# Second attention of a two-layer encoder: three small moves in the order of its steps

## The chip, the cores and the metric

The kernel runs on one core of a Trainium2 chip. The metric is device time in microseconds (us). The core has a matrix engine (PE, with its weight loads as PEld), a vector engine (DVE), a scalar engine (ACT), a general engine (POOL) and queues that issue transfers (DMAs), here nearly all on SP. Each engine runs its own instructions in order, and semaphores hold an instruction until what it needs is done. Matrix products land in PSUM, eight banks of 128 x 512 f32; everything else on chip lies in SBUF.

## The reference

Two layers act on x of 1024 tokens by 1024. Layer 0 is dilated window attention. Layer 1, where the change lies, is latent attention with 16 heads (64 plus 32 rotary columns for the scores, 64 for the values):

```python
    cq, ckv, k_rope, gate = jnp.split(
        u @ w_in, [Q_LORA_RANK, Q_LORA_RANK + KV_LORA_RANK, Q_LORA_RANK + KV_LORA_RANK + QK_ROPE_DIM], axis=-1)
    q = (rmsnorm(cq, q_norm) @ w_uq).reshape(B, S, N_HEADS_B, QK_NOPE_DIM + QK_ROPE_DIM)
...
    kv = (rmsnorm(ckv, kv_norm) @ w_ukv).reshape(B, S, N_HEADS_B, QK_NOPE_DIM + V_HEAD_DIM)
...
    q_rope = rope(q_rope, cos[:, None], sin[:, None])
    k_rope = rope(k_rope, cos, sin)
...
        s = (jnp.einsum('bqhd,bkhd->bhqk', qn, k_nope)
             + jnp.einsum('bqhd,bkd->bhqk', qr, k_rope)).astype(jnp.float32) * scale
        p = jax.nn.softmax(s, axis=-1).astype(v.dtype)
        return jnp.einsum('bhqk,bkhd->bqhd', p, v)
...
    y = o * jax.nn.silu(gate)
    return y @ w_out
```

After each layer x becomes LayerNorm(sqrt(2) * x + gate_c * mixer(u)).

## The kernel before

Every f32 operand of a product is split into a high part (fp32r) and a low part, and a product is three matmuls: high by high, low by high, high by low (`mm3`, lines 93 to 95). A split is a cast on ACT (high) and a subtraction on DVE or POOL (low).

`layer_b_attention` sweeps 64 work items, w = 0 to 63, in one loop with two more turns (w = 64 = `nw`, and 65). One turn is a cycle: w // 4 is the head, w // 8 = p the pair of heads, r = w % 8 the place in the pair. A cycle holds 256 queries of a head as two halves a. In each cycle PE does in this order: scores of half 0 (`full`, `small`, into `s`), the transposes of the previous item's probabilities (`turned`, into `t`), scores of half 1, transposes again, any up-projection (into `m`), and last `values(w - 2)`, the product with V (into `o`). DVE does: `osum` of the previous cycle, the row maximum `mb` of half 0 (line 1452), two low splits `ptl` (line 1491), `mb` of half 1, two more `ptl`. ACT does the high splits `pth`, the exponentials `pr`, and the copy of `o` to `osum` (line 1525). POOL multiplies the result into `gT` (line 1529) and, for every second cycle, by the reciprocal of the softmax denominator (`normalise`, line 1535), which travels through DRAM (`den_d`, `rden`, lines 1515 and 1516).

The order on PE, SP, ACT and DVE is the order in which the code is written; only POOL's is chosen by a scheduler. Four PSUM banks (`mbank`: `t`, `m` and `o`) turn in a ring: each allocation waits until the one four before it has been read. So `values(w - 2)`, and an up-projection in front of it, wait until DVE has done the first `ptl` of the same cycle or the second.

`b_weights(p)` splits the up-projection weights of pair p: a cast to `wuh` on ACT (line 1210), a subtraction to `wul` on POOL (line 1211), and then `b_wload(p + 1)` queues the next raw weights on SP (line 1197, `wuraw`), which overwrite the tile that the split has read. Pair p + 2 is split at r = 7 of pair p. For p + 2 even its first reader is `b_turn` (rotary part) at r = 0 of the next pair, one cycle later; its rotary product is multiplied on DVE (line 1334, `ab`) by tables `tab` that `b_tabs(0)` queues on SP at r = 7 (line 1315). For p + 2 odd the first reader comes at r = 3.

In the last pair (p = 7) the output weights are loaded and split: `b_wo_split(r - 1)` for r = 1 to 4 with its low part on POOL (`wl`, line 106, 128 x 1024). `b_yt(b, 0)` splits a tile of y^T: a cast on ACT (line 1649) and a subtraction on DVE whose two inputs both lie in SBUF (line 1650, `ytb`). Tiles 0, 1, 2 are split at r = 5, 6, 7, tile 3 and 4 in cycle 64. `b_out_blocks(i, blocks)` adds products of y^T and output weights into output rows i (`po`), 6 matmuls a block. In cycle 64 the four blocks of i = 0 stand so: block 0, transposes, block 1, transposes' splits, `values(62)`, blocks 2 and 3; then cycle 65 has `values(63)`.

Of the kernel before, what the change touches and what calls it, by code (L numbers as in the profile page):

```python
# [28 lines left out]
NPAIR_B = 8  # L29
# [41 lines left out]
class Trunk:  # L71
# [1349 lines left out]
    def layer_b_attention(self):  # L1421
# [4 lines left out]
        def full(w, a):  # L1426

            hd, t = w // 4, 2 * (w % 4)
            (qa, qb, q3), k = self.q[hd], self.kb[hd % 3]
            ts = slice((t + a) * P, (t + a) * P + P)  # L1430
            for n, (q, kk) in enumerate(((qa, k[0]), (qb, k[1]))):
                for j in range(2):
                    ks = slice(j * 512, j * 512 + 512)
                    nc.tensor.matmul(sc[w][a][:, ks], q[:, ts], kk[:, ks], start=n == a == 0, stop=n == a == 1)  # L1434
            if a and w % 4 == 3:
                self.q.pop(hd)

        def small(w):

            hd, t = w // 4, w % 4  # L1440
            q3 = self.q[hd][2]
            for g in range(4):
                rows = slice(32 * g, 32 * g + 32)
                ks = slice((g % 2) * 512, (g % 2) * 512 + 512)
                nc.tensor.matmul(  # L1445
                    sc[w][g // 2][:, ks], q3[rows, t * P : t * P + P], self.kr[rows, :],
                    start=g >= 2, stop=g < 2, tile_position=(32 * g, 0),
                )

        def maximum(w, a):  # L1450
            m = mx[w, a] = self.M.tile([P, 4], F32, tag="mb", bufs=4, name=self.nm("mb"))
            nc.vector.tensor_reduce(m[:, 0:1], sc[w][a], axis=AX.X, op=ALU.max, negate=True)  # L1452

        def expo(w, a):
            hd, t = w // 4, 2 * (w % 4) + a
            if t == 0:
                dens[hd] = self.M.tile([P, 8], F32, tag="den", bufs=3, name=self.nm("den"))
            pr = prs[w, a] = self.ht(F32, "pr")
            nc.scalar.activation(  # L1459
                pr, sc[w][a], AF.Exp, bias=mx.pop((w, a))[:, 0:1], accum_out=dens[hd][:, t : t + 1]  # L1460
            )
            if a:
                sc.pop(w)

        def reciprocal(w):
            d = dens[w // 4][:, 2 * (w % 4) - 2 : 2 * (w % 4) + 2]
            nc.vector.reciprocal(d, d)

        def turned(w, a):
            pr = prs.pop((w, a))  # L1470
            tb[w, a] = []
            for j in range(2):
                t = self.mbank("t")
                for c in range(4):
                    kt = 4 * j + c
                    nc.tensor.transpose(t[:, c * P : c * P + P], pr[:, kt * P : kt * P + P], self.ident)  # L1476
                tb[w, a].append(t)
# [4 lines left out]
        def high(w, a):  # L1482
            if a == 0:
                pts[w] = [(self.gt(F32R, "pth"), self.gt(F32R, "ptl")) for _ in range(2)]
            for j in range(2):
                nc.scalar.copy(part(w, a, j, 0), tb[w, a][j].rearrange("p (k q) -> p k q", k=4))  # L1486

        def low(w, a):
            for j, t in enumerate(tb.pop((w, a))):
                src = t.rearrange("p (k q) -> p k q", k=4)  # L1490
                nc.vector.tensor_tensor(part(w, a, j, 1), src, f32(part(w, a, j, 0)), op=ALU.subtract)  # L1491

        def values(w):
            hd = w // 4
            po = ob[w] = self.mbank("o")
            x = [(kt, x) for kt in range(8) for x in range(2)]
            for n, (kt, i) in enumerate(x):
                v = self.vq[hd // 4][kt // 2][:, (kt % 2) * 512 + (hd % 4) * P : (kt % 2) * 512 + (hd % 4) * P + P]
                c = (kt % 4) * 256
                nc.tensor.matmul(po[:, 0:256], v, pts[w][kt // 4][i][:, c : c + 256], start=n == 0, stop=n == 15)  # L1500
            pts.pop(w)
            if w % 16 == 15:
                self.vq.pop(hd // 4)
            if w % 2:
                nc.tensor.transpose(po[0:4, 256:384], dens[hd][:, 2 * (w % 4) - 2 : 2 * (w % 4) + 2], self.ident)
# [25 lines left out]
        def normalise(v):  # L1531
            hd = v // 2
            mine = slice(64 * (hd % 2), 64 * (hd % 2) + 64)
            g = self.gT[hd // 2][mine, v % 2 * 512 : v % 2 * 512 + 512]
            nc.gpsimd.tensor_tensor(g, g, rden.pop(v)[mine, :], op=ALU.mult)  # L1535
# [5 lines left out]
        for w in range(nw + 2):  # L1541
            p, r = divmod(w, 8)
            now, old = w < nw, 1 <= w <= nw
            more = p + 1 < NPAIR_B
            if now:
                sc[w] = [self.PB.tile([P, 1024], F32, tag="s", bufs=2, name=self.nm("s")) for _ in range(2)]
                full(w, 0)
                small(w)
            if w == nw:
                self.b_out_blocks(0, range(1))  # L1550
            if old:
                turned(w - 1, 0)
            if now:
                maximum(w, 0)
            if old:
                high(w - 1, 0)
                low(w - 1, 0)
                if w % 2 == 0:
                    reciprocal(w - 1)
            if now:  # L1560
                expo(w, 0)
                full(w, 1)
                maximum(w, 1)
            if old:
                turned(w - 1, 1)
                high(w - 1, 1)
                low(w - 1, 1)
            if r == 7 and p % 2 == 0 and p + 2 < NPAIR_B:
                self.tabs = {}
                self.b_tabs(0)  # L1570
            if r == 0 and p % 2 and more:
                self.b_tabs(1)

            splits = []
            if p % 2 == 0 and now and r < 2:
                splits += [self.b_v(p // 2, j) for j in (2 * r, 2 * r + 1)]
            if more and r == 3:
                self.b_heads(p + 1)
            if more and 3 <= r <= 6:
                splits.append(self.b_qk(p + 1, "kqkq"[r - 3], (r - 3) // 2))  # L1580
            if more and p % 2 and r < 2:
                turn, store = self.b_turn(p + 1, r)
                splits.append(turn)
                rot.append((w + 1, store))
            late = splits.pop() if w >= 8 and r == 1 and p % 2 == 0 and splits else None
            if w >= 2:
                for f in splits:
                    f()
            if now:
                expo(w, 1)  # L1590
            if w < 2:
                for f in splits:
                    f()
            if more and r == 5:
                self.b_rotary(p + 1)
            if w == nw:
                self.b_out_blocks(0, range(1, 2))
            if w >= 2:
                values(w - 2)
                output(w - 2)  # L1600
            if late:
                late()

            while rot and rot[0][0] <= w:
                rot.pop(0)[1]()
            if w == 1:
                self.b_weights(1)
            if r == 7 and p + 2 < NPAIR_B:
                self.b_weights(p + 2)
            if r == 5 and p % 2 and more:  # L1610
                self.b_vweights((p + 1) // 2)
            if p == 7:
                if r < 4:
                    self.b_wo_load(r)
                if 1 <= r <= 4:
                    self.b_wo_split(r - 1, nc.gpsimd)
                if r >= 5:
                    self.b_yt(r - 5, 0)
                if r == 7:
                    for b in range(4, 8):  # L1620
                        self.b_wo_load(b)
            if w == nw:
                self.b_yt(3, 0)
                self.b_rows()
                self.b_out_blocks(0, range(2, 4))
                for b in (4, 5):
                    self.b_wo_split(b, nc.vector)
                    if b == 4:
                        self.b_yt(b, 0)
            if w == nw + 1:  # L1630
                self.b_out_blocks(1, range(4))
            if w >= 5 and w % 2:
                normalise((w - 5) // 2)
# [225 lines left out]
```

## Time and profile before

| what | us |
|---|---|
| median of 3 runs (1326.19 to 1332.42) | 1326.89 |
| the profiled execution's own time | 1328.96 |
| its span | 1327.2 |
| PE busy with matmuls in the span | 1305.0 (98%) |
| DVE / ACT / POOL busy | 858.4 / 745.8 / 392.4 |

The second attention runs from about 760 us to 1235 us of the span, the output products from there to the end. TensorE's granted clock is full (1.00) in all of it. The busy share says little here: with PE at 98% only what PE waits for can be gained, and what makes it wait longer is lost.

### The profile page before, as it was taken

The numbers are of one execution on the slowest core, as the hardware profiler recorded it, in microseconds if no ns is written. First come the engines' busy times: TensorE is split into PE (matmuls) and PEld (weight loads), VectorE is DVE, ScalarE is ACT, GpSimd is POOL, SyncE is SP. The second block draws the span as 40 slices with busy tenths as digits, with TensorE's granted clock in tenths as the row PEclk, the third lists the DMA queues.
The fourth block names the chain that finished last, engine by engine and source line by source line (L and its number), as shares of the span: only waits on it lengthen the run. The fifth ranks groups of instructions, "written<-read, shape, count | busy, mean of one in ns | idle before, by whom it ended". The sixth has DMA issues, their size and how long they took to land.

```text
span 1327.2 us, 20680 instructions
## 1 busy us (share of the span) xinstructions
PE 1305.0 (98%) x7435; PEld 1100.5 (83%) x7435; DVE 858.4 (65%) x1502; ACT 745.8 (56%) x1519; POOL 392.4 (30%) x399
## 2 busy tenths in 40 slices
PE   9999999999999999999999999999999999999997
PEld 6888888888888888888998878788888888878886
DVE  7654445445445435646754358888888888878896
ACT  5665456554443432435742277777777777778521
POOL 0332133223222267702742101521332142124200
PEclk9999999999999999999999999999999999999999
DMA  9413121113243246545134124462552544340531
GB/s 366 159 31 70 29 64 40 48 40 113 77 148 130 91 124 167 191 150 185 61 114 133 41 69 108 122 154 57 138 131 66 134 120 116 70 126 26 215 127 64
DMA packets 71967, 146.45 MB, mean 110 GB/s; under 512 B 11148, under 2 KB 25789, under 8 KB 71864
## 3 DMA queue, kind: packets, MB, share of 16 engines
q1 hardware_dynamic: 69196, 139.75, 35.7%
q0 software_dynamic: 2048, 5.06, 1.1%
q8 instruction: 59, 0.97, 0.3%
q14 instruction: 44, 0.36, 0.1%
q10 hardware_dynamic: 620, 0.31, 0.1%
HBM read 107.96 MB, written 12.87 MB: 91 GB/s over the span
## 4 chain that ended last, share of the span: by engine, by line
PE 87%; DVE 4%; DMA 4%; ACT 2%; issue 1%; POOL 1%; SPq 0%; ACTq 0%; DVEq 0%; POOLq 0%
PE pj L93 9%; PE pj L95 9%; PE pj L94 9%; PE o L1500 9%; PE s L1434 7%; PE t L1476 7%; PE po L95 5%; PE po L93 5%; PE po L94 5%; PE ip L274 2%; PE t L577 2%; PE pg L93 2%; PE s L1445 2%; PE pg L95 2%; PE pg L94 2%; DVE mb L1452 2%
## 5 line engine op out<-in xcount | busy, mean ns | idle before, releaser
L93 PE MATMUL pj<-uh,wh 128*128 128x512 f32 x528 | 217.2, 411 | 0.7 <-ACT wh L105 0.7
L95 PE MATMUL pj<-uh,wl 128*128 128x512 f32 x528 | 207.1, 392 | 0.0
L94 PE MATMUL pj<-ul,wh 128*128 128x512 f32 x528 | 206.8, 392 | 0.0
L1486 ACT CAST pth<-t 128x512 fp32r<-128x512 f32 x256 | 137.9, 597 | 63.0 <-PE t L1476 62.6
L1452 DVE TENSOR_REDUCE mb<-s 128x1 f32<-128x1024 f32 x128 | 155.2, 1213 | 16.3 <-PE s L1445 15.3
L1491 DVE TENSOR_TENSOR ptl<-t,pth 128x512 fp32r<-128x512 f32 x256 | 164.1, 682 | 1.5 <-ACT pth L1486 0.5
L1459 ACT ACTIVATE pr<-s,mb 128x1024 f32<-128x1024 f32 x128 | 144.9, 1132 | 8.7 <-DVE mb L1452 7.3
L1434 PE MATMUL s<-kb,q 128*128 128x512 f32 x512 | 147.9, 410 | 0.0
L1476 PE MATMUL t<-ident,pr 128*128 128x128 f32 x1024 | 136.2, 276 | 0.7 <-DVE osum L1528 0.7
L106 POOL TENSOR_TENSOR wl<-wraw,wh 128x1024 fp32r<-128x1024 f32 x42 | 106.3, 2537 | 99.3 <-ACT wh L105 73.4
L1476 PEld LDWEIGHTS t<-ident,pr 128*128 128x128 f32 x1024 | 114.5, 141 | 24.8 <-issue 9.1
L1500 PE MATMUL o<-pth,vq 128*128 128x256 f32 x512 | 127.7, 287 | 3.4 <-DVE ptl L1491 3.0
L1500 PE MATMUL o<-ptl,vq 128*128 128x256 f32 x512 | 125.2, 283 | 0.0
L566 ACT ACTIVATE sb<-sb,stat 128x256 f32<-128x256 f32 (+1 forms) x144 | 67.0, 466 | 95.8 <-DVE stat L560 95.7
L95 PEld LDWEIGHTS pj<-uh,wl 128*128 128x128 f32 x528 | 99.1, 188 | 22.2
L93 PEld LDWEIGHTS pj<-uh,wh 128*128 128x128 f32 x528 | 99.7, 189 | 15.1 <-ACT wh L105 1.1
L94 PEld LDWEIGHTS pj<-ul,wh 128*128 128x128 f32 x528 | 99.8, 189 | 13.9
L1500 PEld LDWEIGHTS o<-pth,vq 128*128 128x128 f32 x512 | 97.2, 190 | 7.0 <-DVE ptl L1491 5.5
L1500 PEld LDWEIGHTS o<-ptl,vq 128*128 128x128 f32 x512 | 97.5, 190 | 1.6
L1434 PEld LDWEIGHTS s<-kb,q 128*128 128x128 f32 x512 | 87.0, 189 | 12.6 <-issue 0.2
L1529 POOL TENSOR_TENSOR gT<-osum,gT 64x256 f32<-64x256 f32 x64 | 46.6, 728 | 161.1 <-DVE osum L1528 159.6
L1535 POOL TENSOR_TENSOR gT<-gT,rden 64x512 f32<-64x512 f32 x32 | 41.7, 1302 | 145.8 <-DMA rden<-den_d 135.4
(288 smaller groups left out, 2766.7 us busy)
## 6 DMA issues: line engine op xcount, KB each, us to landing
wraw<-wa SPq DMA_DIRECT2D x36, 512.0 KB
ada<-ada_row SPq DMA_DIRECT2D x64, 256.0 KB
kb<-hl SPq DMA_DIRECT2D x84, 128.0 KB
q<-hl SPq DMA_DIRECT2D x84, 128.0 KB
wraw<-wo_a SPq DMA_DIRECT2D x18, 512.0 KB
ada<-ada_ss SPq DMA_DIRECT2D x16, 512.0 KB
f<-f_d SPq DMA_DIRECT2D x18, 256.0 KB
xr<-x SPq DMA_DIRECT2D x8, 512.0 KB
```

Of the source, the lines that this page charges most:

```text
L93: mm(out, wh, xh, start=start, stop=False)
L94: mm(out, wh, xl, start=False, stop=False)
L95: mm(out, wl, xh, start=False, stop=stop)
L106: (lo_engine or self.nc.gpsimd).tensor_tensor(l[:, :width], raw[:, :width], f32(h[:, :width]), op=ALU.subtract)
L566: nc.scalar.activation(sb[:, a * w : a * w + w], sb[:, a * w : a * w + w], AF.Exp, bias=stat[:, 0, hh, t : t + 1], scale=-1.0, accum_out=s ...
L1434: nc.tensor.matmul(sc[w][a][:, ks], q[:, ts], kk[:, ks], start=n == a == 0, stop=n == a == 1)
L1452: nc.vector.tensor_reduce(m[:, 0:1], sc[w][a], axis=AX.X, op=ALU.max, negate=True)
L1459: nc.scalar.activation(pr, sc[w][a], AF.Exp, bias=mx.pop((w, a))[:, 0:1], accum_out=dens[hd][:, t : t + 1])
L1476: nc.tensor.transpose(t[:, c * P : c * P + P], pr[:, kt * P : kt * P + P], self.ident)
L1486: nc.scalar.copy(part(w, a, j, 0), tb[w, a][j].rearrange("p (k q) -> p k q", k=4))
L1491: nc.vector.tensor_tensor(part(w, a, j, 1), src, f32(part(w, a, j, 0)), op=ALU.subtract)
L1500: nc.tensor.matmul(po[:, 0:256], v, pts[w][kt // 4][i][:, c : c + 256], start=n == 0, stop=n == 15)
```

## The change

Three things move, and nothing is computed more or less. (1) The weights of pair p + 2 are split at r = 6, one cycle sooner. (2) `b_yt` of tiles 0 to 3 comes at r = 4 to 7 of the last pair, tile 4 in cycle 64 ahead of the splits of the output weights. (3) In cycle 64 blocks 1 and 2 stand in front of `values(62)`, block 3 behind it.

```diff
             if w == nw:
-                self.b_out_blocks(0, range(1, 2))
+                self.b_out_blocks(0, range(1, 3))
...
-            if r == 7 and p + 2 < NPAIR_B:
+            if r == 6 and p + 2 < NPAIR_B:
                 self.b_weights(p + 2)
...
-                if r >= 5:
-                    self.b_yt(r - 5, 0)
+                if r >= 4:
+                    self.b_yt(r - 4, 0)
...
             if w == nw:
-                self.b_yt(3, 0)
+                self.b_yt(4, 0)
                 self.b_rows()
-                self.b_out_blocks(0, range(2, 4))
+                self.b_out_blocks(0, range(3, 4))
                 for b in (4, 5):
                     self.b_wo_split(b, nc.vector)
-                    if b == 4:
-                        self.b_yt(b, 0)
```

The built programs show where the instructions land. POOL, cycles 5 to 7 (pair 0; `wul` is the split of pair 2, the two gT<-gT,rden are `normalise`), before:

```order
L1535 TENSOR_TENSOR gT_6064<-gT_6064,rden_7214 64x512
L1529 TENSOR_TENSOR gT_6064<-osum_7309,gT_6064 64x256
L1529 TENSOR_TENSOR gT_6064<-osum_7390,gT_6064 64x256
L1211 TENSOR_TENSOR wul_7399<-wuraw_6846,wuh_7398 128x640
L1535 TENSOR_TENSOR gT_6064<-gT_6064,rden_7392 64x512
```

and now:

```order
L1535 TENSOR_TENSOR gT_6064<-gT_6064,rden_7214 64x512
L1529 TENSOR_TENSOR gT_6064<-osum_7309,gT_6064 64x256
L1211 TENSOR_TENSOR wul_7314<-wuraw_6846,wuh_7313 128x640
L1529 TENSOR_TENSOR gT_6064<-osum_7396,gT_6064 64x256
L1535 TENSOR_TENSOR gT_6064<-gT_6064,rden_7398 64x512
```

The split has moved ahead of one multiplication, not ahead of the `normalise` before it. In pairs 2 and 4 it moves ahead of a `normalise` too. SP at the same place (`wuraw` is the raw weights of pair 3, `tab` the tables of cycles 8 and 9), before:

```order
L1394 DMA q_6980<-hl_7281 64x512
L1315 DMA tab_7365<-qtab 64x512 x4
L1515 DMA den_d<-rden_7392 4x128
L1516 DMA rden_7392<-den_d 64x512
L1197 DMA wuraw_7402<-wu_o 128x384
L1315 DMA tab_7459<-qtab 64x512 x4
```

and now:

```order
L1394 DMA q_6980<-hl_7281 64x512
L1197 DMA wuraw_7317<-wu_o 128x384
L1315 DMA tab_7371<-qtab 64x512 x4
L1515 DMA den_d<-rden_7398 4x128
L1516 DMA rden_7398<-den_d 64x512
L1315 DMA tab_7459<-qtab 64x512 x4
```

The load of raw weights, which waits for the split on POOL, now stands in front of the first tables. DVE from the end of cycle 60 (`osum` is its last instruction there, `mb` and `ptl` belong to cycle 61), before:

```order
L1528 TENSOR_TENSOR osum_12355<-o_12338,osum_12355 64x256
L1452 TENSOR_REDUCE mb_12383<-s_12363 128x1
L1491 TENSOR_TENSOR ptl_12386<-t_12373,pth_12385 128x4x128
L1491 TENSOR_TENSOR ptl_12388<-t_12378,pth_12387 128x4x128
L1452 TENSOR_REDUCE mb_12399<-s_12364 128x1
```

and now:

```order
L1528 TENSOR_TENSOR osum_12355<-o_12338,osum_12355 64x256
L1648 TENSOR_TENSOR ytb_12363<-gT_6064,ytb_12363 128x512
L1452 TENSOR_REDUCE mb_12386<-s_12366 128x1
L1491 TENSOR_TENSOR ptl_12389<-t_12376,pth_12388 128x4x128
L1491 TENSOR_TENSOR ptl_12391<-t_12381,pth_12390 128x4x128
L1452 TENSOR_REDUCE mb_12402<-s_12367 128x1
```

A y^T split stands in front of the first maximum of cycle 61, where there was none; cycles 62 and 63 begin with such a split in both programs. On ACT the matching cast stands behind the cast of the fourth output weights.

## Rows read from the trace of the kernel before

**Rows 1.** What PE waited for, 826 to 1240 us: total, times, longest.

```profile
PE o L1500 <- DVE ptl L1491: 2.8, 6, 1.3
PE m L95 <- POOL wul L1211: 1.3, 1, 1.3
PE t L1476 <- DVE osum L1528: 0.7, 1, 0.7
PE po L95 <- DVE ytb L1650: 0.4, 1, 0.4
```

**Rows 2.** Timeline, cycle 8's rotary product: start, us, engine, line, [idle before <- releaser].

```profile
834.33 0.40 PE L94 MATMUL m<-latl,wuh 128*128 128x512 f32 x1
...
836.03 0.19 PEld L95 LDWEIGHTS m<-lath,wul 128*128 128x128 f32 x1 [1.73 <-POOL wul L1211]
836.03 0.50 PE L95 MATMUL m<-lath,wul 128*128 128x512 f32 x1 [1.30 <-POOL wul L1211]
...
836.60 0.39 PE L94 MATMUL m<-latl,wuh 128*128 128x512 f32 x1
...
836.83 0.39 PE L95 MATMUL m<-lath,wul 128*128 128x512 f32 x1
```

**Rows 3.** Line 1211's own view: weight loads that waited for it (us, times).

```profile
  PEld m L95: 2.6, 3
```

**Rows 4.** Timeline of POOL, 831 to 836 us.

```profile
831.58 1.28 POOL L1535 TENSOR_TENSOR gT<-gT,rden 64x512 f32<-64x512 f32 x1 [13.15 <-DMA rden<-den_d]
832.93 1.43 POOL L1529 TENSOR_TENSOR gT<-osum,gT 64x256 f32<-64x256 f32 x2
834.44 1.54 POOL L1211 TENSOR_TENSOR wul<-wuraw,wuh 128x640 fp32r<-128x640 f32 x1
```

**Rows 5.** Timelines of SP, DVE, PE, cycles 7 to 9; then windows (last: DMA share, GB/s).

```profile
832.92 2.52 SPq L1315 DMA_DIRECT2D tab<-qtab  x4
...
837.26 1.29 DVE L1334 TENSOR_TENSOR ab<-m,tab 128x512 f32<-128x512 f32 x2 [0.55 <-PE m L95]
...
841.79 1.29 DVE L1491 TENSOR_TENSOR ptl<-t,pth 128x512 fp32r<-128x512 f32 x2
...
843.08 0.47 PE L93 MATMUL m<-lath,wuh 128*128 128x512 f32 x1
...
837.00:837.50 0.50, 0.50 (x5) 0.46 (x5) 0.24 (x1) 0.00 (x0) 0.00 (x0) 1.00 0.00 0
```

**Rows 6.** Timeline at the turn from cycle 60 to cycle 61.

```profile
1206.19 1.06 ACT L105 ACTIVATE wh<-woraw 128x1024 fp32r<-128x1024 f32 x1
...
1206.89 1.22 DVE L1452 TENSOR_REDUCE mb<-s 128x1 f32<-128x1024 f32 x1 [0.25 <-PE s L1445]
1207.41 2.39 POOL L106 TENSOR_TENSOR wl<-woraw,wh 128x1024 fp32r<-128x1024 f32 x1
...
1209.44 0.36 PE L1500 MATMUL o<-pth,vq 128*128 128x256 f32 x1
```

**Rows 7.** Timelines of POOL and DVE behind the heads: the two splits meet.

```profile
1239.72 2.49 POOL L106 TENSOR_TENSOR wl<-woraw,wh 128x1024 fp32r<-128x1024 f32 x1 [0.33 <-ACT wh L105]
...
1240.14 2.62 DVE L1650 TENSOR_TENSOR ytb<-gT,ytb 128x512 fp32r<-128x512 f32 x1 [0.21 <-ACT ytb L1649]
```

**Rows 8.** Timeline of cycle 62, which begins with a y^T split already.

```profile
1211.79 0.37 ACT L1525 COPY osum<-o 64x256 f32<-64x256 f32 x1
...
1213.13 1.17 DVE L1650 TENSOR_TENSOR ytb<-gT,ytb 128x512 fp32r<-128x512 f32 x1 [0.18 <-ACT ytb L1649]
...
1216.08 0.39 PE L1500 MATMUL o<-pth,vq 128*128 128x256 f32 x1 [0.19 <-DVE ptl L1491]
...
1219.08 0.36 ACT L1525 COPY osum<-o 64x256 f32<-64x256 f32 x1
```

**Rows 9.** Timeline of PE, block 3 in cycle 64.

```profile
1233.39 0.40 PE L94 MATMUL po<-wl,ytb 128*128 128x512 f32 x1
...
1234.23 0.50 PE L95 MATMUL po<-wh,ytb 128*128 128x512 f32 x1 [0.44 <-DVE ytb L1650]
```

## The prediction, made blind

> **What bounds the kernel.** I read what PE waited for first, over the stretch that the change touches. The view is short: the waits add up to 5.2 us in 414 us [rows 1]. So PE sets the end, and the change can give back no more than the waits it removes. Two of the four rows are its targets: the wait of an up-projection for the weight split `wul` (1.3 us) and that of an output block for a y^T split (0.4 us). A third row, `values` waiting for `ptl`, is the one that the change can make longer, since what is put on DVE in front of `mb` delays `ptl`. Next I read the timelines around each of the three places, to see which engine is late and what is queued there.
>
> **Part 1, weights one cycle sooner.** The price in the trace: the matmul of line 95 starts 1.70 us after the one of line 94, where the undisturbed pitch is 0.23 (836.60 to 836.83), so 1.47 us are lost in cycle 8 [rows 2]. The weight load there stood idle 1.73, and 0.26 of that cost nothing. All three such loads (pairs 2, 4 and 6) idled 2.6 us [rows 3]; the other two share 0.87, of which 2 x 0.26 cost nothing, so 0.35 us.
>
> What is won in those two: there the split moves ahead of a `normalise` and is ready a whole cycle sooner, so I take the 0.35 whole. In cycle 8 it is different. POOL did not start `wul` late because ACT was late, but because it stood 13.15 us in front of a `normalise` whose `rden` came late from DRAM [rows 4]. The new order puts `wul` ahead of one multiplication only, and that `normalise` is still in front. Its DMA is issued ahead of everything that moves, so it lands as before. The split gains one multiplication, half of 1.43: it ends at 835.2 instead of 835.98, and PE gains 0.74 of its 1.47.
>
> What is added: the raw-weight load moves past four `tab` loads on SP and waits for that same split. Behind it are queued the tables for cycle 8. They began at 832.92 and took 0.63 each to issue; now the load starts at 835.2, the tables at about 835.85. The fourth began its issue at 834.8 and no DMA moved anything from 837.0 on, so it landed within 2.2 us [rows 5]. Now the second lands at 838.7, the fourth at 839.9, and DVE's pair of multiplications, which began at 837.26 when the product was there, ends at 840.55 instead of 838.55. Behind it stand `osum` (256 columns; about 0.4, an estimate from the 0.65 of a `ptl` of 512), `mb` (1.22) and the first `ptl` (0.65) [rows 5, 6]: done at about 842.8. The next product on PE needs that bank; it began at 843.08, now it could at 842.34, so it waits about 0.5. Net gain in cycle 8: 0.2. Bounds: 1.47 gained if nothing of this counts, 2.0 lost if the late tables and what follows them on SP hold POOL and then ACT as in the worst such place of the trace, where a 0.7 and a 1.3 us wait on PE stand next to each other [rows 1].
>
> The cast on ACT also moves. In cycle 60 a longer cast (1.06 us) stands in the same place, in front of the next `pth`, and PE's `values` behind it began without a wait [rows 6]. So it costs nothing; if that gap were full it would cost at most that 1.06 in each of six cycles. In pairs 3, 5 and 7 the split has no reader for cycles: nothing won, nothing lost.
>
> **Part 2, one more y^T split within the heads.** Four splits now stand within the heads, not three, and the added one comes at the end of cycle 60. That is the cycle in which POOL makes its last `wl` split, 1207.41 to 1209.80 [rows 6]. The ACT cast for y^T stands behind the ACT cast for `wh`, which also releases POOL; so POOL is always first. What happens then is seen once in the trace: POOL began such a split at 1239.72, DVE a y^T split at 1240.14, and that took 2.62 us, ending 0.55 after POOL's (1242.76 and 1242.21) [rows 7]. In cycle 62 the same instruction took 1.17 [rows 8]. I read it as DVE held until POOL is through. The Trainium skill says so too (page "SBUF — State Buffer", section "Who interferes with whom"): a DVE instruction with two SBUF inputs and a GpSimd instruction that reads SBUF exclude each other for the whole of the first, and whoever issues first goes first. By that rule the sum below stands; were the 2.62 a chance delay of ACT's, it would be the first rival.
>
> So the added split ends at 1209.80 + 0.55 = 1210.35. Behind it on DVE wait `mb`, which began at 1206.89, and `ptl`. In cycle 62 `values` began 1.78 us after its split's end (1214.30 to 1216.08), and ACT's copy to `osum` at the end of that cycle 4.78 after it (1219.08) [rows 8]. So cycle 61's `values` begin at 1212.13 instead of 1209.44: PE stands 2.7 us. And ACT's copy, on which cycle 62's chain hangs, comes at 1215.13 instead of 1211.79, 3.3 us later. Cycles 62 and 63 have the split in both kernels and are already bound by this chain (PE waits there), so they pass the 3.3 on and give nothing back. Bounds: 0 if all of it hides, 3.5 if `mb` itself sets the rest (1210.35 less 1206.89).
>
> **Part 3, cycle 64.** Block 3 waited for its y^T tile: 0.84 between two matmuls where 0.23 is the pitch, 0.6 lost [rows 9]. Tile 3 is now split a cycle sooner, and block 3 comes behind `values(62)`: I take the 0.6 whole. Blocks 1 and 2 need tiles split in cycles 61 and 62. The same matmuls run in another order, at no cost. DVE has one y^T split less between 1233 and 1237, so the output weights behind it are no later.
>
> **The sum**, against the profiled execution (1328.96, of it 1327.2 span): +3.3 - 0.6 - 0.35 - 0.2 = +2.1 us, 1331.1. That execution stands 2.07 above the median of the runs; on the median of 1326.89 it is 1329.0. About 0.5%, 6.6 us, is what a measurement of this kernel can tell from no change, so this is "the same".
>
> **The rivals.**
> First, DVE is not held: the added split starts when ACT's cast is done (`wh` ends at 1207.25, a cast half as wide adds about 0.5: 1207.8), and takes the 1.17 of its neighbours. It ends at 1209.0, ACT's copy comes at 1213.8, 2.0 late: +2.0 - 1.15 = +0.85, 1327.7. For it: other splits within the heads are not long. Against it: none of them meets a `wl` on POOL.
> Second, faster: the added split hides, and all three weight waits go: -1.47 - 0.35 - 0.6 = -2.4, 1324.5. For it: in cycle 61 PE did not wait for DVE. Against it: cycles 62 and 63 did as soon as they had such a split.
> Third, SP becomes the one that is late: the held load makes tables, denominators and rotary rows late after cycle 8 and costs 2.0 there instead of the gain of 0.2: +4.3, 1331.2. For it: SP's DMAs stand back to back there. Against it: DVE and PE have slack in a cycle with a product.
> Fourth, over the bound: in pairs 1, 3 and 5 the two weight loads now also stand in front of a denominator. If each late denominator holds POOL, and so ACT, at 2.0 as in the worst place, that is three times 2.0 on top of the third rival: +10.3, 1337.2. It decides if POOL takes a `normalise` ahead of a multiplication that ACT's tile needs; POOL's new order does not do that there.
>
> **The numbers.** Forecast 0.5, first rival 0.2, second 0.1, third 0.15, fourth 0.05. The range takes in the forecast, the first and third rival and half of the second, with a run's scatter of about 1 us: 1325.2 to 1332.0. Faster by over 0.5% needs more than all shown waits: 0.01. Slower by over 0.5% is the fourth rival: 0.05. The rest, 0.94, is the same.
>
> **What would show it.** Right: a y^T split of about 2.5 us near 1207.8 that ends just behind POOL's `wl`, and behind it a wait of PE's `values` for `ptl` of 2 to 3 us in cycle 61; a wait for `wul` in cycle 8 that shrinks but stays, near 0.6; none in pairs 4 and 6; no wait of an output block for `ytb`; DVE's multiplication by `tab` in cycle 8 beginning 1 to 2 us after its product. Wrong: a short split there, or a `values` of cycle 61 without a wait (part 2); no wait for `wul` at all, or a new one of ACT for POOL in cycles 8 to 10 (part 1).

## The result, and the profile after

| what | before | after |
|---|---|---|
| median of 20 runs each, us | 1329.35 (1326.19 to 1332.97) | 1332.17 (1329.43 to 1336.52) |
| ratio after to before, 95% interval | 1 | 1.0022 (1.0014 to 1.0031) |
| the profiled execution's own time, us | 1328.96 | 1330.68 |
| its span, us | 1327.2 | 1328.9 |

The changed kernel is slower by 2.9 us (1.9 to 4.1), 0.2% and so within the 0.5% called "the same". The forecast of a difference was +2.1. The forecast of a time, 1329.0 with a range up to 1332.0, was too low: the median of the kernel before, which it was set on, rose from 1326.89 in three runs to 1329.35 in twenty.

The waits of PE over 826 to 1240 us, as in [rows 1]:

```profile
PE o L1500 <- DVE ptl L1491: 5.7, 7, 2.4
PE m L93 <- DVE ptl L1491: 1.0, 1, 1.0
PE m L95 <- POOL wul L1211: 0.6, 1, 0.6
```

The wait for `ytb` is gone, and so is the one of a transpose for `osum`. The wait for `wul` has halved. In their place stand 2.9 us more of `values` waiting for `ptl`, and an up-projection that waits 1.0.

**Cycle 8** (answers [rows 2] and [rows 4]), timelines of PE and POOL:

```profile
834.44 0.40 PE L94 MATMUL m<-latl,wuh 128*128 128x512 f32 x1
835.41 0.50 PE L95 MATMUL m<-lath,wul 128*128 128x512 f32 x1 [0.57 <-POOL wul L1211]
```

```profile
831.65 1.27 POOL L1535 TENSOR_TENSOR gT<-gT,rden 64x512 f32<-64x512 f32 x1 [13.11 <-DMA rden<-den_d]
833.00 0.73 POOL L1529 TENSOR_TENSOR gT<-osum,gT 64x256 f32<-64x256 f32 x1
833.82 1.55 POOL L1211 TENSOR_TENSOR wul<-wuraw,wuh 128x640 fp32r<-128x640 f32 x1
```

POOL still stands 13.11 us in front of `normalise`. The split now follows one multiplication instead of two, ends at 835.37, and PE's step from line 94 to line 95 is 0.97 us instead of 1.70. **Cycle 9** pays for it (answers [rows 5]); timelines of SP, DVE, PE:

```profile
835.39 0.37 SPq L1197 DMA_DIRECT2D wuraw<-wu_o  x1
835.86 2.43 SPq L1315 DMA_DIRECT2D tab<-qtab  x4
```

```profile
839.14 0.69 DVE L1334 TENSOR_TENSOR ab<-m,tab 128x512 f32<-128x512 f32 x1 [2.37 <-DMA tab<-qtab]
840.50 0.69 DVE L1334 TENSOR_TENSOR ab<-m,tab 128x512 f32<-128x512 f32 x1 [0.67 <-DMA tab<-qtab]
```

```profile
843.68 0.50 PE L93 MATMUL m<-lath,wuh 128*128 128x512 f32 x1 [0.98 <-DVE ptl L1491]
```

SP holds the raw load until the split has ended (835.39), the tables begin 2.9 us later than before (835.86 against 832.92), and DVE waits for them twice. Windows of a quarter of a us (the last two columns are the share of the DMA engines and GB/s) show when the tables' last bytes moved:

```profile
839.75:840.00 0.25, 0.25 (x6) 0.20 (x3) 0.08 (x1) 0.00 (x0) 0.00 (x0) 1.00 0.07 17
840.00:840.25 0.25, 0.25 (x4) 0.25 (x4) 0.00 (x0) 0.00 (x0) 0.00 (x0) 1.00 0.00 0
```

No transfer moved anything from 840.00 on, and yet DVE went on only at 840.50.

**Cycles 60 and 61** (answers [rows 6]), timelines of POOL, DVE, PE:

```profile
1206.67 2.37 POOL L106 TENSOR_TENSOR wl<-woraw,wh 128x1024 fp32r<-128x1024 f32 x1
```

```profile
1206.96 2.63 DVE L1648 TENSOR_TENSOR ytb<-gT,ytb 128x512 fp32r<-128x512 f32 x1 [1.06 <-ACT ytb L1647]
1209.52 1.21 DVE L1452 TENSOR_REDUCE mb<-s 128x1 f32<-128x1024 f32 x1
```

```profile
1211.38 0.39 PE L1500 MATMUL o<-pth,vq 128*128 128x256 f32 x1 [2.36 <-DVE ptl L1491]
1218.61 0.39 PE L1500 MATMUL o<-pth,vq 128*128 128x256 f32 x1 [0.76 <-DVE ptl L1491]
```

The added y^T split lasts 2.63 us, ends at 1209.59, 0.55 after POOL's `wl` (1209.04), and `values` of cycle 61 stands 2.36. In cycle 64 the matmuls of block 3 follow each other at 0.23 (answers [rows 9]):

```profile
1235.60 0.40 PE L93 MATMUL po<-wh,ytb 128*128 128x512 f32 x1
1235.83 0.40 PE L94 MATMUL po<-wl,ytb 128*128 128x512 f32 x1
1236.07 0.39 PE L95 MATMUL po<-wh,ytb 128*128 128x512 f32 x1
```

**Where the difference sits, cycle by cycle.** From the timeline of PE I took the start of the small scores (line 1445) in each cycle. The table has the length from one such start to the next, in us, of each kernel's profiled execution; all cycles left out agree within 0.3. "Start" is where cycle 0 begins, "rest" what follows the start of cycle 63. The runs are explained below; the first two have the same instruction order.

| kernel | start | 8 | 9 | 24 | 26 | 40 | 56 | 57 | 61 | 62 | rest |
|---|---|---|---|---|---|---|---|---|---|---|---|
| before | 778.7 | 9.06 | 7.60 | 7.86 | 6.10 | 7.68 | 8.65 | 6.21 | 6.20 | 6.56 | 108.1 |
| norm_later | 778.4 | 9.05 | 7.60 | 8.50 | 6.48 | 8.51 | 8.45 | 6.20 | 6.20 | 6.55 | 108.0 |
| after | 778.8 | 8.33 | 8.86 | 7.50 | 6.10 | 7.50 | 7.92 | 6.21 | 8.83 | 7.13 | 107.3 |
| after_again | 777.7 | 7.97 | 8.75 | 7.50 | 7.26 | 7.50 | 7.85 | 6.21 | 10.36 | 6.52 | 107.3 |
| weights_only | 777.7 | 7.97 | 8.88 | 7.51 | 6.10 | 7.50 | 7.79 | 6.21 | 6.20 | 6.56 | 108.1 |
| load_late | 778.5 | 7.74 | 7.60 | 7.51 | 6.10 | 7.50 | 9.85 | 6.22 | 6.21 | 6.56 | 108.1 |
| yt_only | 779.9 | 9.28 | 7.60 | 7.73 | 6.38 | 8.32 | 9.75 | 6.21 | 10.22 | 6.56 | 107.3 |
| yt_first | 781.0 | 9.85 | 7.60 | 7.53 | 6.10 | 7.99 | 7.75 | 6.20 | 6.50 | 7.13 | 107.2 |
| yt_early | 778.1 | 8.88 | 7.60 | 8.05 | 6.10 | 8.35 | 8.04 | 7.20 | 6.21 | 6.54 | 107.3 |
| pool_yt | 781.6 | 8.57 | 7.60 | 7.50 | 7.18 | 7.51 | 7.76 | 6.20 | 6.21 | 6.10 | 106.3 |
| pool_fixed | 779.4 | 7.51 | 7.58 | 7.51 | 6.93 | 7.50 | 6.10 | 6.20 | 6.21 | 6.50 | 108.1 |
| best | 781.0 | 7.50 | 7.59 | 7.51 | 6.14 | 7.51 | 6.10 | 6.21 | 6.20 | 6.10 | 106.2 |
| best_old_weights | 778.1 | 7.50 | 7.59 | 7.51 | 7.43 | 7.51 | 6.10 | 6.21 | 6.21 | 6.10 | 106.3 |
| after_fixed | 779.5 | 7.50 | 7.72 | 7.51 | 6.10 | 7.50 | 6.10 | 6.21 | 10.28 | 6.52 | 107.3 |

After against before: -0.73 + 1.26 in cycles 8 and 9, -0.36 - 0.18 in 24 and 40, -0.73 in 56, +2.63 + 0.57 in 61 and 62, -0.8 in the rest, +0.1 at the start: +1.8 with the roundings, and the spans differ by 1.7. The -0.73 of cycle 56 can be credited to no part: with the scheduler's order on POOL this cycle took 7.75 to 9.75 us in the five executions without part 1 and 7.76 to 9.85 in the five with it.

### The profile page after: what moved, and what is told of

It is laid out like the page before. It is cut to its first block, busy times and chain, and to the rows that moved or that the text cites. A ratio compares the mean times of both kernels' runs of the same rounds, so it can differ in the third digit from the quotient of the medians.

```text
span 1328.9 us, 20687 instructions
## 1 busy us (share of the span) xinstructions
PE 1305.1 (98%) x7435; PEld 1102.4 (83%) x7435; DVE 854.2 (64%) x1502; ACT 746.8 (56%) x1519; POOL 391.4 (29%) x399
## 4 chain that ended last, share of the span: by engine, by line
PE 87%; DVE 5%; DMA 3%; ACT 2%; issue 1%; SPq 1%; POOL 0%; DVEq 0%; ACTq 0%; POOLq 0%
PE pj L93 9%; PE pj L95 9%; PE pj L94 9%; PE o L1500 8%; PE s L1434 7%; PE t L1476 6%; PE po L94 5%; PE po L93 5%; PE po L95 5%; PE ip L274 2%; PE t L577 2%; PE pg L93 2%; DVE mb L1452 2%; PE pg L94 2%; PE pg L95 2%; PE s L1445 2%
## 5 line engine op out<-in xcount | busy, mean ns | idle before, releaser
L106 POOL TENSOR_TENSOR wl<-wraw,wh 128x1024 fp32r<-128x1024 f32 x42 | 106.3, 2537 | 101.4 <-ACT wh L105 72.0
```

The source lines that it names most:

```text
L106: (lo_engine or self.nc.gpsimd).tensor_tensor(l[:, :width], raw[:, :width], f32(h[:, :width]), op=ALU.subtract)
```

## The experiments

**Part 1 alone (weights_only).**

```diff
-            if r == 7 and p + 2 < NPAIR_B:
+            if r == 6 and p + 2 < NPAIR_B:
                 self.b_weights(p + 2)
```

> Part 1 alone (weights one cycle sooner). Read against the kernel before by the start of each cycle's scores on PE. Theory: cycle 8 is 0.73 shorter (the wait for wul shrinks from 1.3 to 0.6), cycle 9 is 1.26 longer (tables late behind the held load), cycles 24 and 40 are 0.36 and 0.2 shorter; sum -0.03 at cycle 56. If the 0.73 won in cycle 56 by the changed kernel comes from this part too, then -0.76 at cycle 61 and at the end, else -0.03. Rival: the late tables are a matter of that one execution, cycle 9 keeps its 7.60 and the part gives -1.3.

Measured: 1330.21 (1326.78 to 1333.48) against 1329.33 for before, ratio 1.000 (0.9987 to 1.0013). PE's timeline has both waits:

```profile
834.03 0.50 PE L95 MATMUL m<-lath,wul 128*128 128x512 f32 x1 [0.21 <-POOL wul L1211]
842.33 0.50 PE L93 MATMUL m<-lath,wuh 128*128 128x512 f32 x1 [1.01 <-DVE ptl L1491]
```

Cycle 8 won 1.09 and cycle 9 lost 1.28. Part 1 is worth nothing there; what it wins lies in cycles 24 and 40, too little for the times of the runs to show.

**Part 1 with the raw load left in its place (load_late).** Only the split moves; the load stands behind the tables on SP again.

```diff
-        self.b_wload(p + 1)
+        if p < 2:
+            self.b_wload(p + 1)
...
-            if r == 7 and p + 2 < NPAIR_B:
+            if r == 6 and p + 2 < NPAIR_B:
                 self.b_weights(p + 2)
+            if r == 7 and p + 2 < NPAIR_B:
+                self.b_wload(p + 3)
```

> Part 1, but the load of the next raw weights stays where it was on SP, behind the tables and the denominators of r = 7; only the split itself comes at r = 6. Theory: cycle 8 still 0.73 shorter (POOL stands in front of the late normalise as ever), cycle 9 unchanged at 7.60, cycles 24 and 40 shorter by 0.36 and 0.2: -1.3 in all, and no wait of DVE for tab. Rival (the loss of cycle 9 comes from the split on POOL or the cast on ACT, not from SP's order): cycle 9 still longer by about 1.2.

Measured: 1328.34 (1325.91 to 1333.2), ratio 0.9997 (0.9986 to 1.0008). Cycle 9 is back at 7.60 with cycle 8 at 7.74: the loss in cycle 9 comes from SP's order, not from the split on POOL or the cast on ACT, which moved here too. Cycle 56, which no edit touches, was 1.20 longer. PE's timeline and the granted clock (the column behind five engines with their instruction counts) show why:

```profile
1174.33 0.66 PE L1477 MATMUL t<-ident,pr 128*128 128x128 f32 x4 [0.44 <-DVE osum L1529]
1176.31 0.58 PE L1501 MATMUL o<-pth,vq 128*128 128x256 f32 x1 [1.32 <-DVE ptl L1492]
1176.69 0.42 PE L1501 MATMUL o<-ptl,vq 128*128 128x256 f32 x1
1176.90 0.41 PE L1501 MATMUL o<-pth,vq 128*128 128x256 f32 x1
```

```profile
1172.00:1176.00 4.00, 2.55 (x17) 1.86 (x15) 2.09 (x3) 2.01 (x5) 1.73 (x3) 1.00 0.35 73
1176.00:1180.00 4.00, 3.69 (x17) 3.69 (x18) 3.24 (x6) 2.94 (x6) 1.30 (x1) 0.57 0.47 164
```

After two waits that stand in before too, the clock fell to 0.57 in the mean of 1176 to 1180: products with V of 0.21 each instead of 0.12, TensorE's lower level.

**Parts 2 and 3 alone (yt_only).**

```diff
             if w == nw:
-                self.b_out_blocks(0, range(1, 2))
+                self.b_out_blocks(0, range(1, 3))
...
-                if r >= 5:
-                    self.b_yt(r - 5, 0)
+                if r >= 4:
+                    self.b_yt(r - 4, 0)
...
-                self.b_yt(3, 0)
+                self.b_yt(4, 0)
                 self.b_rows()
-                self.b_out_blocks(0, range(2, 4))
+                self.b_out_blocks(0, range(3, 4))
...
-                    if b == 4:
-                        self.b_yt(b, 0)
```

> Parts 2 and 3 alone (four y^T splits within the heads, two output blocks ahead of values(62)). Theory: nothing moves up to cycle 60; cycles 61 and 62 are longer by 2.6 and 0.6; 0.8 comes back in cycle 64; end at +2.4. Rival (the cost in the heads comes from what part 1 changed in SP's queue): cycle 61 longer by less than 1.

Measured: 1331.73 (1330.73 to 1335.47), ratio 1.0022 (1.0011 to 1.0032), as the whole change. PE waits 2.36 us in cycle 61 again, but the cycle is 10.22 long and not 8.83: the clock fell behind the wait (granted 0.69 in the mean of 1216 to 1220). In cycle 64 no block waits, and the rest is 0.8 shorter.

**The y^T split ahead of the weight split (yt_first).** As yt_only, with the added split written in front of `b_wo_split`, so that DVE comes before POOL.

```diff
+                if r >= 4:
+                    self.b_yt(r - 4, 0)
                 if 1 <= r <= 4:
                     self.b_wo_split(r - 1, nc.gpsimd)
-                if r >= 5:
-                    self.b_yt(r - 5, 0)
```

> Parts 2 and 3, but at r = 4 the y^T split stands in front of the split of the output weights, so that DVE's subtraction is ready before POOL's wl has begun and meets POOL's short multiplication (0.73) alone. Theory (DVE is held while POOL reads SBUF): DVE's split takes about 1.2 instead of 2.6 and ends at about 1208 instead of 1210.3, cycle 61 is longer by 0.3 to 0.6 and cycle 62 by 0.3 to 0.6, end at +0.2 (from -0.1 to +0.5). Rival (any fourth split costs this much, because DVE's chain of cycles 61 to 63 has no room): cycles 61 and 62 together still longer by 2.5 or more, end at +2.

Measured: 1329.8 (1327.13 to 1335.66), ratio 1.0011 (0.9997 to 1.0025). DVE and POOL:

```profile
1208.86 1.24 DVE L1648 TENSOR_TENSOR ytb<-gT,ytb 128x512 fp32r<-128x512 f32 x1
```

```profile
1208.82 0.73 POOL L1529 TENSOR_TENSOR gT<-osum,gT 64x256 f32<-64x256 f32 x1 [1.11 <-DVE osum L1528]
1209.85 2.51 POOL L106 TENSOR_TENSOR wl<-woraw,wh 128x1024 fp32r<-128x1024 f32 x1 [0.30 <-ACT wh L105]
```

The same split takes 1.24 instead of 2.63 when it comes ahead of `wl`; POOL's is 0.14 longer than in the changed kernel. Cycles 61 and 62 together grow by 0.87 instead of 3.20 (the times of the runs, 1.0011 here and 1.0022 in yt_only, do not tell the two kernels apart; the cycles do). So the stall of cycle 61 is the meeting with `wl`, and the first rival's small price belongs to a split that does not stand behind it.

Even the 1.24 is not the split's own time: POOL's short multiplication began 0.04 us ahead of it, and the split ended at 1210.10, again 0.55 after POOL's 1209.55. A split that begins while POOL does nothing is shorter, as this one of the changed kernel behind the heads, and there POOL's multiplication, 0.05 later, takes 1.24 instead of 0.73 (DVE, POOL):

```profile
1240.75 0.69 DVE L1648 TENSOR_TENSOR ytb<-gT,ytb 128x512 fp32r<-128x512 f32 x1
```

```profile
1240.80 1.24 POOL L1529 TENSOR_TENSOR gT<-osum,gT 64x256 f32<-64x256 f32 x1 [3.36 <-DVE osum L1528]
```

Over all fourteen profiled executions 86 y^T splits on DVE began while an instruction of POOL (0.72 to 3.26 us long) was running, and every one of them ended 0.55 us after POOL's; every other one took 0.68 or 0.69.

**The added split at the end of cycle 56 (yt_early)**, where POOL splits nothing; the other three splits within the heads come in the cycles of before, the output blocks as in part 3:

```diff
+                if r == 0:
+                    self.b_yt(0, 0)
...
                 if r >= 5:
-                    self.b_yt(r - 5, 0)
+                    self.b_yt(r - 4, 0)
```

> Before with the output-block order of the change, but the added y^T split stands at the end of cycle 56, where GpSimd has no weight split, and the other three at the ends of cycles 61 to 63 as before. Theory (the 2.6 us of cycle 61 are VectorE's split held behind GpSimd's `wl`): VectorE's `ytb` of cycle 56 takes 1.17 to 1.25 us instead of 2.63; cycle 57 grows by 0 to 0.7, cycles 61 to 63 stand as in the kernel before (6.20, 6.56, 7.1), the wait for `ytb` in cycle 64 (0.44) is gone, so that these parts together come to -0.8 to 0 us. Rival (any fourth split costs what the change's cost, wherever it stands): a cycle after 56 grows by over 2 us and the whole by 2 to 3 us.

Measured: 1329.29 (1327.2 to 1333.41) against 1328.51, ratio 1.0004 (0.999 to 1.0019). The split takes 1.13, cycles 61 and 62 are as before, the rest is 0.8 shorter, and cycle 57 is 0.99 longer, more than the 0 to 0.7 expected:

```profile
1182.26 1.13 DVE L1650 TENSOR_TENSOR ytb<-gT,ytb 128x512 fp32r<-128x512 f32 x1 [0.23 <-ACT ytb L1649]
```

A split of DVE in front of `mb` cost PE some 0.4 to 1.0 us in each of these places, where it met POOL's short multiplication; it is the meeting with `wl` that costs 2 to 3 more.

**`normalise` written a cycle later (norm_later).**

```diff
-            if w >= 5 and w % 2:
-                normalise((w - 5) // 2)
+            if w >= 6 and w % 2 == 0:
+                normalise((w - 6) // 2)
+            if w == nw + 1:
+                normalise(30)
```

> Before with one edit: each `normalise` (GpSimd's multiplication that waits for the row of denominators to come back from DRAM) is issued one cycle later, so that one more multiplication of an attention output, and in cycle 7 the split of the weights, stand ahead of it in GpSimd's queue. Theory (the waits of cycles 8, 40 and 56 are GpSimd's queue standing behind a denominator that is late, and differ from execution to execution with that transfer): cycle 8 falls from 9.06 to about 7.7 us, and cycle 56 from 8.65 to between 6.2 and 7.3 (ScalarE's copy there no longer waits 3.1 us); together -2.5 to -3.8 us. Rival (the waits are the transfers' own and come back one cycle later): cycles 8 and 56 lose under 0.5 us together, or cycles 9, 10, 57 or 58 give it back.

Measured: 1328.61 (1327.19 to 1330.83), ratio 1.0004 (0.9995 to 1.0012). It says nothing of the theory: POOL's order is the scheduler's, which puts each `normalise` behind two multiplications whatever the code says, and every engine's order was that of the kernel before. What it gives is a second execution of that order: cycles 24 and 40 are 0.64 and 0.83 longer than in the first, with nothing changed.

**POOL in the order of the code (pool_fixed).**

```diff
-ORDERED = FIXED | {mybir.EngineType.Activation, mybir.EngineType.DVE}
+ORDERED = FIXED | {mybir.EngineType.Activation, mybir.EngineType.DVE, mybir.EngineType.Pool}
```

> Before with one edit: GpSimd's instructions in the second attention stand in the order in which the code is written instead of the scheduler's, so that each `normalise` stands behind four multiplications of attention outputs instead of two, and the weight split of cycle 7 ahead of the `normalise` that waits for its denominators. (In the run with `normalise` written a cycle later the scheduler had put it back: every engine's order was that of the kernel before.) Theory (cycles 8, 24, 40 and 56 wait for GpSimd's queue, which stands behind a late denominator): cycle 8 falls from 9.06 to about 7.7 us, cycles 24 and 40 to 7.5, cycle 56 from 8.65 to between 6.2 and 7.4; together -3 to -4 us. Rival (these waits are the transfers' own): cycles 8 and 56 together lose under 0.5 us, or the cycles after them give it back.

Measured: 1325.58 (1323.78 to 1328.03) against 1329.12, ratio 0.9969 (0.9957 to 0.9981). Cycle 8 fell to 7.51, cycle 56 to 6.10. POOL around cycle 55, before and then in this kernel:

```profile
1173.40 1.27 POOL L1535 TENSOR_TENSOR gT<-gT,rden 64x512 f32<-64x512 f32 x1 [12.90 <-DMA rden<-den_d]
1174.74 0.74 POOL L1529 TENSOR_TENSOR gT<-osum,gT 64x256 f32<-64x256 f32 x1
```

```profile
1166.54 0.73 POOL L1529 TENSOR_TENSOR gT<-osum,gT 64x256 f32<-64x256 f32 x1 [5.24 <-DVE osum L1528]
1173.22 0.73 POOL L1529 TENSOR_TENSOR gT<-osum,gT 64x256 f32<-64x256 f32 x1 [5.96 <-DVE osum L1528]
1174.02 1.30 POOL L1535 TENSOR_TENSOR gT<-gT,rden 64x512 f32<-64x512 f32 x1
```

Before, POOL stood 12.90 us in front of a `normalise`. The multiplication behind it ran at 1174.74 (at 1166.54 in the new order), and ACT's next copy in the kernel before waited for that:

```profile
1175.51 0.36 ACT L1525 COPY osum<-o 64x256 f32<-64x256 f32 x1 [3.10 <-POOL gT L1529]
```

In the new order two multiplications go first, and the denominator has landed when its turn comes. Over the whole kernel line 1535's own view counts POOL's idle time for that transfer, before and in this kernel (us, times):

```profile
  DMA rden<-den_d: 135.4, 27
```

```profile
  DMA rden<-den_d: 0.5, 1
```

**The changed kernel once more (after_again).**

> The changed kernel once more, to see what of it repeats. Theory: cycle 61 again holds a wait of 2.36 us and VectorE's split of 2.6 us, cycle 9 again a wait of 1.0; the time of GpSimd's `rden` and so cycles 8, 40 and 56 differ from the first profile by up to 1 us. The clock may fall after the wait of cycle 61 (then that cycle is 10.2 us, as in the run of the y^T parts alone) or not (8.8). Ratio to the kernel before between 1.001 and 1.003. Rival (the first profile was a chance): cycle 61 under 7 us, or cycle 9 at 7.6.

Measured: 1331.51 (1330.59 to 1335.03), ratio 1.0026 (1.0017 to 1.0036). The wait of 2.37 in cycle 61 and the 0.90 in cycle 9 repeat. This time the clock fell; windows of the first execution, then of this one, and its matmuls:

```profile
1208.00:1212.00 4.00, 1.64 (x14) 1.41 (x13) 4.00 (x5) 1.27 (x4) 1.04 (x1) 1.00 0.00 0
1212.00:1216.00 4.00, 4.00 (x31) 3.29 (x31) 3.01 (x5) 3.75 (x8) 0.45 (x1) 1.00 0.02 5
```

```profile
1208.00:1212.00 4.00, 1.63 (x11) 1.40 (x10) 4.00 (x5) 1.61 (x4) 0.67 (x1) 0.91 0.00 0
1212.00:1216.00 4.00, 4.00 (x22) 3.33 (x20) 2.27 (x4) 2.84 (x7) 0.00 (x0) 0.66 0.02 4
```

```profile
1211.01 0.38 PE L1500 MATMUL o<-pth,vq 128*128 128x256 f32 x1 [2.37 <-DVE ptl L1491]
...
1211.81 0.41 PE L1500 MATMUL o<-pth,vq 128*128 128x256 f32 x1
1212.02 0.41 PE L1500 MATMUL o<-ptl,vq 128*128 128x256 f32 x1
```

The granted clock was 1.00 and 1.00 in the one, 0.91 and 0.66 in the other, and the cycle was 8.83 and 10.36 us for the same wait.

**Low halves of the y^T splits on POOL (pool_yt)**, on top of load_late, with the added split at the end of cycle 56 and the block order of part 3 (lines stand one further down):

```diff
+                if r == 0:
+                    self.b_yt(0, 0, nc.gpsimd)
                 if r >= 5:
-                    self.b_yt(r - 5, 0)
+                    self.b_yt(r - 4, 0, nc.gpsimd)
...
-    def b_yt(self, b, hf):
+    def b_yt(self, b, hf, lo=None):
...
-        nc.vector.tensor_tensor(y[:, 512:1024], src, f32(y[:, 0:512]), op=ALU.subtract)
+        (lo or nc.vector).tensor_tensor(y[:, 512:1024], src, f32(y[:, 0:512]), op=ALU.subtract)
```

> Candidate: part 1 with the load left at the end of cycle 7, the block order of part 3, the added y^T split at the end of cycle 56, and the low halves of the y^T splits of cycles 56 and 61 to 63 on GpSimd instead of VectorE. Theory: cycle 8 at 7.7 and cycle 9 at 7.6 us (-1.3 against the kernel before); the waits of 0.19, 0.72 and 0.72 us for `ptl` in cycles 61 to 63, which stand behind VectorE's split, are gone (-1.0 to -1.6), the wait for `ytb` in cycle 64 too (-0.4 to -0.8); together -2.7 to -3.7 us, cycle 56 aside. Rival (GpSimd's split holds VectorE's sums of two SBUF inputs or comes too late): waits of PE of over 0.5 us in cycles 62 to 64, and a gain of under 1.5 us.

Measured: 1325.31 (1324.01 to 1328.77), ratio 0.9982 (0.9972 to 0.9992). Cycles 61 and 62 are 6.21 and 6.10, and the rest is 1.8 shorter than before. POOL has time for it, directly behind its multiplication:

```profile
1215.07 0.72 POOL L1530 TENSOR_TENSOR gT<-osum,gT 64x256 f32<-64x256 f32 x1 [3.31 <-DVE osum L1529]
1215.75 1.29 POOL L1653 TENSOR_TENSOR ytb<-gT,ytb 128x512 fp32r<-128x512 f32 x1
```

Cycle 8 was 8.57, not the 7.7 expected: this execution's denominator was late again (a wait of 0.8 for `wul`).

**Both (best), and both without part 1 (best_old_weights).** best is pool_yt with POOL's order as written. best_old_weights takes part 1 out of it, so that weights and loads stand as in the kernel before.

> Candidate: the kernel of the low y^T splits on GpSimd (which was 3.2 us under the kernel before) with GpSimd's order as written besides. Theory: what cycle 8 and 56 still hold there (8.57 and 7.76 us) falls to about 7.7 and 6.2 to 7.4; -0.8 to -2.4 us against that kernel, -4 to -5.5 against the kernel before. Rival: as written, GpSimd's y^T splits stand behind other work and the last block waits; then PE's waits in cycles 62 to 64 come back (0.4 to 1.5 us) and the gain is lost.

Measured: 1324.45 (1322.25 to 1325.01) against 1329.12, ratio 0.9958 (0.9946 to 0.997): 5.6 us (4.0 to 7.2) faster than the kernel before. Cycles 8 and 56 are 7.50 and 6.10, and the block does not wait.

> The best kernel so far without part 1: the weights are split at the end of cycle 7 and loaded there, as in the kernel before. Theory (with GpSimd's order as written nothing is left for part 1 to win): cycle 8 at 7.5, cycle 9 at 7.6, cycle 56 at 6.1, cycles 61 and 62 at 6.2 and 6.1 us, and the same time as the best within 0.7 us, so 4 to 5.5 us under the kernel before. Rival (part 1 still pays): cycles 8, 24 and 40 hold a wait for `wul` again, 0.5 to 2 us slower than the best.

Measured: 1322.92 (1322.26 to 1324.64) against 1329.26, ratio 0.995 (0.9937 to 0.9963): 6.6 us (4.9 to 8.4) faster than the kernel before. Its slowest run is also under the changed kernel's fastest (1329.43). Cycles 8, 24 and 40 hold no wait for `wul`; over 826 to 1240 PE waits for one thing alone:

```profile
PE o L1500 <- DVE ptl L1491: 1.7, 4, 1.1
```

So nothing of part 1 was needed once POOL stood right.

**The changed kernel with POOL's order as written (after_fixed)**, the one-line edit of pool_fixed on the changed kernel.

> The changed kernel with GpSimd's order as written. Theory: the gains of that order and the losses of the change add up: cycle 8 at 7.5 and cycle 56 at 6.1 us, but cycle 9 still 8.8 (the load of raw weights in front of the tables) unless the split, which no longer waits, lets the load go a cycle sooner (then 7.6); cycle 61 still 8.8, or 10.3 with a fall of the clock. Ratio to the kernel before 0.998 to 1.0005. Rival (the stall of cycle 61 comes from the scheduler's order too): cycle 61 under 7 us.

Measured: 1327.38 (1324.93 to 1328.89), ratio 0.998 (0.9969 to 0.9991), 4.5 us above best_old_weights. Cycle 61 is 10.28: its stall does not come from the scheduler's order. Cycle 9 is 7.72. The split no longer waits, so SP's load does not either, and the tables behind it begin 1.4 us sooner than in the changed kernel (834.45 against 835.86), in an execution that lies 0.7 later there:

```profile
833.76 0.59 SPq L1197 DMA_DIRECT2D wuraw<-wu_o  x1
834.45 2.43 SPq L1315 DMA_DIRECT2D tab<-qtab  x4
```

## Why the prediction was right and wrong

**The step that failed is the last of the sum:** "on the median of 1326.89 it is 1329.0", and with it "a run's scatter of about 1 us". Three runs of the kernel before had given 1326.19, 1326.89 and 1332.42; twenty give 1329.35, with eleven of them outside 1327.9 to 1332.3. The profiled execution's 1328.96 was nearer to it than the median that I moved the sum to; +2.1 on 1329.35 would have been 1331.5, inside the range. The range was too narrow for the same reason. The 0.5% that a measurement was said to need was too coarse as well: twenty runs each told 0.2% from nothing. The scatter itself can be seen in the table: the two executions of one instruction order (before, norm_later) differ by 0.64 in cycle 24 and 0.83 in cycle 40, and cycle 0 starts between 777.7 and 781.6 in kernels that are the same up to there. That the difference of +2.1 lies inside the measured 1.9 to 4.1 is in part luck, as errors of both signs stand in it: part 1's two terms below, and a fall of the clock that has no term.

**Part 2 was right in its mechanism.** The split was forecast at 2.5 us, ending 0.55 after `wl`, at 1210.35, with a stall of 2 to 3 in cycle 61; it took 2.63, ended 0.55 after, and the stall was 2.36. As the Trainium skill says (page "SBUF — State Buffer", section "Who interferes with whom"), the one that issues first goes first. The traces agree, both ways: 86 of 86 splits ended 0.55 after the POOL instruction that came first, and POOL's multiplication took 1.24 instead of 0.73 behind a split. What the prediction missed is that the 1.17 of cycle 62, which it set against the 2.62, is such a held split too, behind POOL's multiplication; alone a split takes 0.69. POOL in the kernel before, 0.55 ahead of that split's end at 1214.30:

```profile
1213.02 0.72 POOL L1529 TENSOR_TENSOR gT<-osum,gT 64x256 f32<-64x256 f32 x1 [3.23 <-DVE osum L1528]
```

The term of +3.3 was 3.20 in the first profile (2.63 + 0.57). It lacked the clock: in three of the four executions with this stall (yt_only, after_again, after_fixed) it fell, and the two cycles grew by 4.0 to 4.1: 1.4 to 1.5 more in cycle 61, of which cycle 62 gave 0.6 back.

**Part 3** won 0.8, forecast 0.6.

**Part 1 misread one landing and took one term from a single execution.** The gross gain of cycle 8 was 0.73, forecast 0.74. The late tables were put at 0.5 and cost 1.26. The step that was wrong is "no DMA moved anything from 837.0 on, so it landed within 2.2 us": it took the last byte that moved for the landing. The bytes came as forecast: the fourth table, whose issue began at about 837.7 (835.86 and three quarters of 2.43), had moved by 840.00, where the prediction has 839.9. But DVE was let go at 840.50, 2.8 after the issue; in weights_only too nothing moved after 838.6 and DVE went on at 839.14. In the kernel before no row could show this half us, as DVE did not wait there. The sign set for this step, DVE 1 to 2 us behind its product, was missed: it idled 2.37 for the first table alone. DVE's pair ended at 841.19 instead of 840.55, and PE waited 0.98. And the 0.35 of cycles 24 and 40 was taken from one execution: over the five with the old order of weights (before, norm_later, yt_only, yt_first, yt_early) these two cycles take 15.5 to 17.0 together, with part 1 always 15.0, so it wins 0.5 to 2.0. Over the same runs cycles 8 and 9 together take 16.48 to 17.45 without part 1 and 16.72 to 17.19 with it: nothing.

**The rivals.** The first (DVE not held) falls with the 2.63; the 1.17 that it took for a free split was a held one. The second needed the stall to hide. The third put 2.0 on cycle 8 for SP; SP is late there, as it says, at 1.26. The fourth did not come: no new wait in pairs 1, 3 and 5. One premise did not hold, that no more can be won than the waits that PE shows: cycle 56 showed waits of 0.7 and 1.3 in the kernel before and became 2.55 shorter in pool_fixed (8.65 to 6.10).

**What stays open.** Adding means of the table, part 1 wins about 1, part 2 costs 3.2 or 4.1 and part 3 wins 0.8: +1.4 to +2.3, and 2.9 (1.9 to 4.1) was measured. The runs of the parts add up better, though with wide intervals: weights_only 0 (-1.7 to 1.7), yt_only 2.9 (1.5 to 4.3). Which executions lose the clock, and how often, I have from profiled ones alone, one per kernel. Cycle 26 is 6.1 in eight executions, 6.4 to 6.5 in two and 6.9 to 7.4 in four; I did not follow it.

## What to carry to other kernels

Look at what stands in front of a late step before you move the step: here an engine stood 13 us before a multiplication that waited for a transfer, and freeing that queue by one line won more than moving what was queued behind it, and made the move needless. Before a step goes on an engine, ask what another engine does at that very moment: the same split cost 0.9 or 3.2 us, by which of the two came first. When a transfer's delay is read from a trace, take the moment at which the engine that waits goes on, not the last byte that moved. Where a scheduler sets an engine's order, look for an edit in the built order, and set a forecast on a median of more than three runs.

## What the runs showed of the hardware

DVE's subtraction of two SBUF inputs (128x512) takes 0.69 us when POOL is idle as it begins. When a POOL instruction is running, it ends 0.55 us after that one, in 86 of 86 cases; the time that the trace gives for it is then mostly waiting. POOL behind such a subtraction is held too (1.24 instead of 0.73).

The engine that waits for a transfer goes on later than its last bytes move: DVE at 840.50, the bytes by 840.00.

A wait of 2.4 us on PE can cost more than itself. Behind it the granted clock fell to the lower level (1.2 GHz) in three of four executions: products with V came every 0.21 us instead of 0.12 for some 3 us, and then it was full again (2.4 GHz); the two cycles cost 0.8 to 0.9 us more for it. In cycle 56 the waits of 0.4 to 0.7 and of 1.3 us stand together in four executions. In two the clock fell (load_late, yt_only: 9.85 and 9.75 us), in two it did not (before, norm_later: 8.65 and 8.45). Behind the 1.3 alone it never fell, in six. PE's busy share shows nothing of it, as the slower matmuls count as busy; the granted clock of a narrow window does.
